# Two mixer layers: the gate projections in three float32r passes instead of plain float32

## The chip, the cores and the metric

One core of one Trainium2 chip. The time is the device time of one execution in microseconds (us), as a median over runs; lower is better. The engines are PE (TensorE, matrix products), DVE (VectorE), ACT (ScalarE), POOL (GpSimd) and SP (SyncE, which issues all transfers here).

## What is computed

A hybrid encoder trunk of two layers, 256 tokens of 1024 channels. Each layer is a SwiGLU FFN, then the mixers, then a second FFN. In the mixers one input projection feeds three branches (RWKV-7, Hyena long convolution, Mamba-2 SSD) and the gates:

```python
proj = h @ w_in
ya = rwkv7_mixer(proj[..., :o1], ...) @ pa_w
yb = hyena_mixer(proj[..., o1:o2], ...) @ pb_w
yc = ssd_mixer(proj[..., o2:o3], ...) @ pc_w
gates = jax.nn.sigmoid(proj[..., o3:]).reshape(bsz, L, N_BRANCH, D_MODEL)
merged = gates[:, :, 0] * ya + gates[:, :, 1] * yb + gates[:, :, 2] * yc
return merged @ w_out
```

## The kernel before

Activations lie with channels on the 128 partitions and tokens along the row, so 1024 channels are eight tiles of 128x256. A projection tile of 128 output channels is eight products, each with a 128x128 piece of a 512 KB weight tile. Per mixer layer there are 63 such tiles: 15 for RWKV, 12 for Hyena, 12 for SSD, 24 for the gates (eight per branch), and one narrow tile for SSD's dt.

There are two ways to multiply. `plain` loads a weight tile into the ring `raw` (four slots), and the product is float32; its two matmul records are named `psd<-hhi,raw`, since the input tiles carry the name `hhi`. `unit` loads into the same ring and then splits the weights into a high part `whi` (ACT, L279, two of 128x512) and a low part `wlo` (DVE, L309, two of 128x512, raw minus `whi`); `mm3` then makes three float32r passes: high by high, high by low, low by high. The FFN, the merges and the output projection use `unit`; all input projections of the mixers use `plain`. Not all of the tiles are made at the same place: the first few of a layer are made early, behind the preceding FFN.

The order on each engine comes from a scheduler that simulates the program and fills each in-order engine's queue; each engine then runs its own queue in that order, and waits on semaphores. `bank` and `dbank` give PSUM banks (`psd`, three of them, for projections; `psm` and `pss` for the rest).

`mixers` goes through RWKV first: `rw_proj` projects and shifts (the shifts on DVE read the bank twice, then it is free), `rw_keys` and `rw_scores` make scaled keys and masked score triangles for two pairs of heads (the masks are DVE multiplications with `cst`), which SP moves through DRAM (`zin`) into the layout in which `rw_invert` inverts them on POOL (some 60 operations, L919 and L921), and back (`zout`). `rw_chain` and `rw_out` then work with 32x32 and 64x64 matmuls that need the inverted triangles. Gate, dt and SSD tiles have no part in that chain, and the scheduler uses them to fill PE. A gate's result goes through ACT (`go`) to DRAM (`gate`) and comes back as `gi` at the merges. `merge` multiplies each branch by its weights and its gate, in the order 2 (SSD), 0 (RWKV), 1 (Hyena). A branch is split for `mm3` by `out_split` into `yx`. Buffers named `arena_0` and `arena_1` are one memory that `take` and `give` cut up; `arena_1` lies in the pool of the phase `q`, which ends with `rw_out(1)`, and the pools `wp` and `lp` open behind it.

## Time and profile before

| | before |
|---|---|
| median of 3 runs | 1668.75 us (1667.75 to 1669.92) |
| profiled execution | 1675.59 us, its span 1673.7 us |
| granted clock of PE, mean | 0.975 |
| busy PE / DVE / ACT / POOL | 94% / 69% / 48% / 16% |
| mixers' projections, layer 0 / layer 1 | about 258 to 565 us / 1073 to 1372 us |

Busy is the time in which an engine works on instructions, as a share of the span. An engine's idle time matters only where it lies in the chain that ends last.

### The profile page before, as it was taken

The page shows a single profiled execution, that of the slowest core. Times are in us where ns is not written, and L with a number is a line of the kernel's source. Part 1 is how long each engine was busy: PE and PEld are TensorE (multiplying, and loading weights), DVE is VectorE, ACT ScalarE, POOL GpSimd, SP SyncE. Part 2 cuts the span into 40 slices and gives each one's busy share as a digit, 9 for nine tenths or more (in the row PEclk, how much of TensorE's full clock was granted, in tenths as well). Part 3 has the DMA queues.
Part 4 walks back from the last instruction along what each step waited for, and adds up shares of the span by engine and source line. Part 5 has one row for each costly group of instructions (what it writes and reads, how often), then busy time and mean ns, then how long its engine had stood idle before and what let it go on. Part 6 is the DMA issues. An engine that isn't in the chain of part 4 may idle for free.

```text
span 1673.7 us, 31929 instructions
## 1 busy us (share of the span) xinstructions
PE 1569.5 (94%) x12118; PEld 1424.0 (85%) x12118; DVE 1150.0 (69%) x2326; ACT 801.3 (48%) x1566; POOL 267.4 (16%) x376
## 2 busy tenths in 40 slices
PE   5999999879998988899999999998999998989996
PEld 2999998768877878899999999877787787989996
DVE  6788856636446677888888887467454557876665
ACT  2655545423243535655575555452424342665554
POOL 0000013567001001100030000348620100030001
PEclk9999999989999999899999999998999999989998
DMA  9898834554548754788869986345555655666663
GB/s 376 305 324 280 282 123 155 129 127 144 169 150 288 242 170 151 282 304 295 266 220 366 315 307 199 120 106 138 156 151 158 223 188 194 189 198 221 222 177 93
DMA packets 157879, 355.74 MB, mean 213 GB/s; under 512 B 55900, under 2 KB 75805, under 8 KB 157470
## 3 DMA queue, kind: packets, MB, share of 16 engines
q1 hardware_dynamic: 157726, 353.71, 64.3%
q8 instruction: 95, 1.56, 0.4%
q14 instruction: 58, 0.48, 0.1%
HBM read 332.11 MB, written 18.91 MB: 210 GB/s over the span
## 4 chain that ended last, share of the span: by engine, by line
PE 66%; DVE 10%; POOL 9%; DMA 7%; ACT 4%; issue 3%; SPq 1%; DVEq 0%; ACTq 0%; POOLq 0%
PE psd L293 57%; PE psm L293 5%; PE pss L293 4%; POOL arena L921 3%; POOL arena L919 3%; DVE arena L282 3%; DVE arena L290 2%; DVE wlo L309 1%; SPq L296 1%; DMA arena<-in_ada 1%; ACT L279 1%; DMA gi<-gate 1%; DMA ada_raw<-in_ada 1%; ACT arena L279 1%; DMA raw<-in_pab 1%
## 5 line engine op out<-in xcount | busy, mean ns | idle before, releaser
L279 ACT ACTIVATE whi<-raw 128x512 fp32r<-128x512 f32 x608 | 370.6, 618 | 328.8 <-PE psd L293 268.2
L309 DVE TENSOR_TENSOR wlo<-raw,whi 128x512 fp32r<-128x512 f32 x608 | 405.1, 676 | 135.1 <-ACT whi L279 120.2
L293 PE MATMUL psd<-hhi,raw 128*128 128x256 f32 x1856 | 435.8, 389 | 0.7 <-DVE arena L290 0.7
L293 PEld LDWEIGHTS psd<-hhi,raw 128*128 128x128 f32 x1856 | 348.9, 192 | 63.3 <-issue 11.6
L293 PE MATMUL psd<-hhi,whi 128*128 128x256 f32 x1360 | 385.4, 285 | 9.9 <-DVE r L290 4.9
L293 PE MATMUL psd<-hhi,wlo 128*128 128x256 f32 x1360 | 384.6, 284 | 1.3 <-DVE wlo L309 1.3
L293 PE MATMUL psd<-hlo,whi 128*128 128x256 f32 x1360 | 385.5, 284 | 0.0
L293 PEld LDWEIGHTS psd<-hhi,whi 128*128 128x128 f32 x1360 | 262.0, 193 | 11.8 <-ACT sg L279 4.6
L293 PEld LDWEIGHTS psd<-hhi,wlo 128*128 128x128 f32 x1360 | 261.9, 193 | 1.6 <-DVE wlo L309 1.5
L293 PEld LDWEIGHTS psd<-hlo,whi 128*128 128x128 f32 x1360 | 262.5, 193 | 0.1
L293 PE MATMUL psd<-alo,whi 128*128 128x256 f32 x704 | 198.7, 282 | 0.0
L293 PE MATMUL psd<-ahi,wlo 128*128 128x256 f32 x704 | 197.8, 281 | 0.0
L293 PE MATMUL psd<-ahi,whi 128*128 128x256 f32 x704 | 197.4, 280 | 0.0
L581 POOL TENSOR_TENSOR r<-r,lmu 128x256 f32<-128x256 f32 x36 | 31.2, 899 | 1020.7 <-ACT lmu L279 841.3
L290 DVE SCALAR_TENSOR_TENSOR ada_raw<-ada_raw,cond 128x1024 f32<-128x1024 f32 x104 | 127.1, 1222 | 20.3 <-DMA ada_raw<-in_ada 20.1
L293 PEld LDWEIGHTS psd<-ahi,wlo 128*128 128x128 f32 x704 | 134.0, 190 | 0.3
L293 PEld LDWEIGHTS psd<-alo,whi 128*128 128x128 f32 x704 | 132.8, 189 | 0.2
L293 PEld LDWEIGHTS psd<-ahi,whi 128*128 128x128 f32 x704 | 132.2, 188 | 0.1
L293 PE MATMUL pss<-arena 128*64 128x128 f32 (+5 forms) x486 | 101.7, 385 | 26.9 <-ACT arena L279 8.6
L279 ACT ACTIVATE arena<-arena 128x512 f32<-128x512 f32 (+4 forms) x108 | 65.8, 619 | 102.5 <-DVE arena L290 35.6
L293 PEld LDWEIGHTS pss<-arena 128*64 128x64 f32 (+3 forms) x486 | 65.4, 195 | 52.1 <-issue 21.0
L293 PE MATMUL psm<-arena 32*32 32x32 f32 (+6 forms) x664 | 64.5, 263 | 28.1 <-DVE arena L290 12.6
(228 smaller groups left out, 2169.9 us busy)
## 6 DMA issues: line engine op xcount, KB each, us to landing
raw<-in_wi SPq DMA_DIRECT2D x176, 512.0 KB, 4.6
raw<-in_win SPq DMA_DIRECT2D x118, 512.0 KB, 3.8
ada_raw<-in_ada SPq DMA_DIRECT2D x104, 512.0 KB, 5.5
raw<-in_wo SPq DMA_DIRECT2D x64, 512.0 KB, 3.8
arena<-in_ada SPq DMA_DIRECT2D x32, 512.0 KB, 5.9
raw<-in_wo SPq DMA_DIRECT2D x32, 384.0 KB, 3.7
raw<-in_pab SPq DMA_DIRECT2D x24, 512.0 KB, 4.3
raw<-in_wout SPq DMA_DIRECT2D x16, 512.0 KB, 4.2
```

Of the source, the lines that this page charges most:

```text
L279: return self.nc.scalar.activation(out=out, in_=in_, func=func, **k)
L282: return self.nc.vector.tensor_tensor(out=out, in0=a, in1=b, op=op)
L290: return self.nc.vector.scalar_tensor_tensor(out=out, in0=a, scalar=s, in1=b, op0=op0, op1=op1, **k)
L293: return self.nc.tensor.matmul(out, lhsT, rhs, start=start, stop=stop, **k)
L296: self.nc.sync.dma_start(out, in_)
L309: return self.act(hi, src, AF.Copy), (eng or self.nc.vector).tensor_tensor(out=lo, in0=src, in1=hi.bitcast(F32), op=SUB)
L581: x = sub_(out=r[:, m, :], in0=r[:, m, :], in1=mu[:], op=SUB)
L919: g.tensor_tensor(out=tv, in0=zw[:, j + 1:32, j:j + 1].to_broadcast([64, n, j]), in1=zw[:, j:j + 1, 0:j].to_broadcast([64, n, j]), op=MUL)
L921: g.tensor_tensor(out=zw[:, j + 1:32, 0:j], in0=zw[:, j + 1:32, 0:j], in1=tv, op=ADD)
```

## The change

The 24 gate tiles of a layer go through `unit` and take three float32r passes over a split input. For that `h_part` splits the eight input tiles into `hlo` (the high part, on ACT) and `hl` (the low part, on DVE), in eight steps. It is written behind `rw_proj(l, 1)`. The SSD outputs stay whole (`sy0`, `sy1`) and are split when they are merged, as the other two branches were; `yx` moves from the pool `pp` to `lp`. All other tiles stay as they were.

```diff
@@ -685,17 +685,25 @@
         self.dense_pair(outs, ws, self.h)
         self.paired = dict(zip(ij, outs))
 
-    def proj(self, l, i):
+    def proj(self, l, i, parted=False):
         if i in self.ready:
             y, b = self.ready.pop(i)
             self.act(y, y, AF.Identity, bias=b)
             return y
         if i in self.paired:
             return self.paired.pop(i)
-        w = self.plain(self.ap["win"][l, i].rearrange("p k c -> p (k c)"))
+        w = (self.unit if parted else self.plain)(self.ap["win"][l, i].rearrange("p k c -> p (k c)"))
         p = self.dbank()
-        self.dense(p[:], w, self.h)
+        self.dense(p[:], w, self.hs if parted else self.h)
         return p
+
+    def h_part(self):
+
+        self.hs = []
+        for x in self.h:
+            hi, lo = self.t("hlo", 256, 8, F32R), self.pt("hl", 256, 8, F32R)
+            self.split(hi[:], lo[:], x)
+            self.hs.append((hi[:], lo[:]))
 
     def shift(self, l, dst, i, spread=False):
 
@@ -1082,7 +1090,7 @@
         self.ya.append(y)
 
     def out_split(self, y):
-        yx = self.pt("yx", [2, 2, 256], 2, F32R)
+        yx = self.lt("yx", [2, 2, 256], 2, F32R)
         self.split(yx[:, 0], yx[:, 1], y)
         return [(yx[:, 0, p, :], yx[:, 1, p, :]) for p in (0, 1)]
 
@@ -1194,7 +1202,7 @@
                             self.mm(py[64 * e:64 * e + 64, p, ts], xd[:, c, d, hs], ws[:, e, n, :], n == 0, n == 2)
                     F(f"sws{t}")
                 F("svb")
-            y = A("sy", 2, 256)
+            y = self.main.take(f"sy{g}", (2, 256))
             for p in (0, 1):
                 j = 2 * g + p
                 self.stt(y[:, p, :], self.sx[:, j, :], self.dh[:, j:j + 1], py[:, p, :], MUL, ADD)
@@ -1208,8 +1216,8 @@
             self.rsqrt(rs)
             for p in (0, 1):
                 self.stt(y[:, p, :], y[:, p, :], self.pc(l, "snw", 2 * g + p), rs, MUL, MUL)
-            self.yc += self.out_split(y)
-            F("scb", "sy", "ssq", "srs", "xd")
+            self.yc.append(y)
+            F("scb", "ssq", "srs", "xd")
 
 
     def hy_sin(self, x):
@@ -1342,7 +1350,7 @@
         for br in (2, 0, 1):
             self.gd[br] = self.dp.tile([128, 8, 256], F32, tag=f"gate{br}", bufs=2, name=f"gate{l}{br}")
             for m in range(8):
-                pg = self.proj(l, 39 + 8 * br + m)
+                pg = self.proj(l, 39 + 8 * br + m, True)
                 go = self.pt("go", 256, 2)
                 self.act(go[:], pg, AF.Tanh, scale=0.5)
                 self.dma(self.gd[br][:, m, :], go[:])
@@ -1372,7 +1380,7 @@
         A = self.A
         with self.phase("q") as pool:
             self.arena_open((self.pp, ARENA), (pool, AHEAD))
-            blk = self.arena.sub("blk", BLK)
+            self.main, blk = self.arena, self.arena.sub("blk", BLK)
             st = [None, None]
             self.gd, self.mh = [None] * 3, []
             self.relief = REL[0]
@@ -1383,6 +1391,7 @@
             self.rw_keys(st[0])
             self.rw_scores(st[0])
             st[1] = self.rw_proj(l, 1)
+            self.h_part()
             self.relief = REL[1]
             self.rw_invert(st[0])
             self.rw_keys(st[1])
@@ -1422,14 +1431,16 @@
                 self.ring = None
             self.mg = self.A("mg", 8, 256)
             self.relief = REL[4]
-            self.merge(l, 2, self.yc, True, False)
+            both = lambda ys: [x for y in ys for x in self.out_split(y)]
+            self.merge(l, 2, both(self.yc), True, False)
+            self.F("sy0", "sy1")
             with self.within(blk):
                 self.hyena(l)
             self.ln_begin(l, 1)
             wout = [self.ap["wout"][l, m].rearrange("p k c -> p (k c)") for m in range(8)]
             ws = [self.unit(u, ahead=NPRE) for u in wout[:NPRE]]
-            self.merge(l, 0, [x for y in self.ya for x in self.out_split(y)], False, False)
-            self.merge(l, 1, [x for y in self.yb for x in self.out_split(y)], False, True)
+            self.merge(l, 0, both(self.ya), False, False)
+            self.merge(l, 1, both(self.yb), False, True)
             self.F("y0", "y1")
             self.relief = REL[5]
             for m in range(8):
```

What moves on the engines, in layer 0. First DVE's start of the mixers: `psd_2963` to `psd_2966` are banks of the projections made early, and the `arena_0` rows are their shifts. Before:

```order
L286 TENSOR_SCALAR a0h_3129<-par_66 128x8
L290 SCALAR_TENSOR_TENSOR arena_0_3094<-psd_2963,par_66,arena_0_3094 128x255
L290 SCALAR_TENSOR_TENSOR arena_0_3094<-psd_2964,par_66,arena_0_3094 128x255
L290 SCALAR_TENSOR_TENSOR arena_0_3094<-psd_2963,par_66,arena_0_3094 128x255
L290 SCALAR_TENSOR_TENSOR arena_0_3094<-psd_2965,par_66,arena_0_3094 128x255
L290 SCALAR_TENSOR_TENSOR arena_0_3094<-psd_2964,par_66,arena_0_3094 128x255
L290 SCALAR_TENSOR_TENSOR arena_0_3094<-psd_2966,par_66,arena_0_3094 128x255
```

and in the changed kernel:

```order
L286 TENSOR_SCALAR a0h_3129<-par_66 128x8
L309 TENSOR_TENSOR hl_3491<-hhi_3029,hlo_3490 128x256
L309 TENSOR_TENSOR hl_3495<-hhi_3032,hlo_3494 128x256
...
L309 TENSOR_TENSOR hl_3519<-hhi_3050,hlo_3518 128x256
L290 SCALAR_TENSOR_TENSOR arena_0_3094<-psd_2963,par_66,arena_0_3094 128x255
L290 SCALAR_TENSOR_TENSOR arena_0_3094<-psd_2964,par_66,arena_0_3094 128x255
L290 SCALAR_TENSOR_TENSOR arena_0_3094<-psd_2965,par_66,arena_0_3094 128x255
L290 SCALAR_TENSOR_TENSOR arena_0_3094<-psd_2966,par_66,arena_0_3094 128x255
L290 SCALAR_TENSOR_TENSOR arena_0_3094<-psd_2963,par_66,arena_0_3094 128x255
L290 SCALAR_TENSOR_TENSOR arena_0_3094<-psd_2964,par_66,arena_0_3094 128x255
```

The eight `hl` rows now stand ahead of the first shift, and the second shift of `psd_2963` is the fifth instead of the third. On ACT the eight `hlo` stand between and behind the rows that make the input tiles, ahead of the first row of the work that follows (`wab`):

```order
L279 ACTIVATE hhi_3044<-r_2099,mod_938 128x256
L279 ACTIVATE hlo_3502<-hhi_3038 128x256
L279 ACTIVATE hlo_3506<-hhi_3041 128x256
L279 ACTIVATE hhi_3047<-r_2099,mod_938 128x256
L279 ACTIVATE hhi_3050<-r_2099,mod_938 128x256
L279 ACTIVATE hlo_3510<-hhi_3044 128x256
L279 ACTIVATE hlo_3514<-hhi_3047 128x256
L279 ACTIVATE hlo_3518<-hhi_3050 128x256
L279 ACTIVATE wab_3052<-psd_2963 128x2
L279 ACTIVATE wab_3056<-psd_2964 128x2
```

before, three rows of `hhi` stood there, and then `wab`. Second, DVE at the score masks of the first pair of heads (`psm_3269` and `pss_3270`, then `psm_3281` and `pss_3282`). Before:

```order
L282 TENSOR_TENSOR arena_1_3095<-arena_0_3094,arena_1_3095 128x512
L290 SCALAR_TENSOR_TENSOR arena_1_3095<-arena_0_3094,arena_1_3095 64x8x64 x4
L282 TENSOR_TENSOR arena_1_3095<-psm_3269,cst 128x512
L282 TENSOR_TENSOR arena_1_3095<-pss_3270,cst 128x512
L282 TENSOR_TENSOR arena_1_3095<-psm_3281,cst 128x512
L282 TENSOR_TENSOR arena_1_3095<-pss_3282,cst 128x512
L282 TENSOR_TENSOR arena_1_3095<-psm_3330,cst 128x512
```

and in the changed kernel:

```order
L282 TENSOR_TENSOR arena_1_3095<-arena_0_3094,arena_1_3095 128x512
L290 SCALAR_TENSOR_TENSOR arena_1_3095<-arena_0_3094,arena_1_3095 64x8x64 x4
L309 TENSOR_TENSOR wlo_4510<-raw_4507,whi_4509 128x512
L309 TENSOR_TENSOR wlo_4514<-raw_4507,whi_4513 128x512
L309 TENSOR_TENSOR wlo_4548<-raw_4545,whi_4547 128x512
L309 TENSOR_TENSOR wlo_4552<-raw_4545,whi_4551 128x512
L282 TENSOR_TENSOR arena_1_3095<-psm_3269,cst 128x512
L282 TENSOR_TENSOR arena_1_3095<-pss_3270,cst 128x512
L309 TENSOR_TENSOR wlo_4586<-raw_4583,whi_4585 128x512
L282 TENSOR_TENSOR arena_1_3095<-psm_3281,cst 128x512
L282 TENSOR_TENSOR arena_1_3095<-pss_3282,cst 128x512
L282 TENSOR_TENSOR arena_1_3095<-psm_3330,cst 128x512
```

Five `wlo` of the gates' weights (tiles `raw_4507`, `raw_4545`, `raw_4583`) have come in ahead of the second pair of masks. Fifteen more stand between the masks and the end of the second pair's scores. Third, PE at the first matmuls that need the first inversion (32x32, `psm_3846` before, `psm_3878` in the changed kernel). `psd_4618` and `psd_4890` are the dt tile, `psd_4654` and `psd_4926` the first SSD tile. Before:

```order
L293 MATMUL psd_4618<-hhi_3050,raw_4616 64x256
L293 MATMUL psd_4654<-hhi_3029,raw_4652 128x256
...
L293 MATMUL psd_4654<-hhi_3038,raw_4652 128x256
L293 MATMUL psm_3846<-arena_1_3095 32x32 x2
L293 MATMUL psd_4654<-hhi_3041,raw_4652 128x256
L293 MATMUL psd_4654<-hhi_3044,raw_4652 128x256
L293 MATMUL psm_3846<-arena_1_3095 32x32 x30
```

and in the changed kernel:

```order
L293 MATMUL psd_4860<-hl_3519,whi_4856 128x256
L293 MATMUL psm_3839<-cst,arena_0_3094 64x64 x16
L293 MATMUL psd_4860<-hlo_3518,wlo_4857 128x256
L293 MATMUL psd_4890<-hhi_3029,raw_4888 64x256
...
L293 MATMUL psd_4926<-hhi_3029,raw_4924 128x256
...
L293 MATMUL psd_4944<-hhi_3029,raw_4942 128x256
...
L293 MATMUL psd_4962<-hhi_3029,raw_4960 128x256
...
L293 MATMUL psd_4962<-hhi_3035,raw_4960 128x256
L293 MATMUL psm_3878<-arena_1_3095 32x32
...
L293 MATMUL psd_4962<-hhi_3038,raw_4960 128x256
L293 MATMUL psm_3878<-arena_1_3095 32x32 x31
```

Ten gates and the dt tile stand ahead of them in both; of the SSD tiles half of the first before, two and three eighths of the third now. Last, ACT where the SSD outputs are split. Before, among the operations of `rw_chain`:

```order
L279 ACTIVATE arena_0_3094<-arena_0_3094 128x256
L279 ACTIVATE yx_4939<-arena_0_3094 128x512
L279 ACTIVATE go_5159<-psd_5150 128x256
...
L279 ACTIVATE arena_0_3094<-psd_5260,par_66 128x256
L279 ACTIVATE yx_5033<-arena_0_3094 128x512
L279 ACTIVATE arena_0_3094,mod_5065<-arena_0_3094 128x1024
```

and in the changed kernel, behind `rw_out(1)`'s last `arena_1` rows and among the first transforms of Hyena (L1309):

```order
L1309 COPY arena_0_3094<-pss_6225 128x512
L279 ACT_TABLE_LOAD
L279 ACTIVATE arena_1_3095<-arena_1_3095 128x512
L1309 COPY arena_0_3094<-pss_6231 128x512
L279 ACT_TABLE_LOAD
L279 ACTIVATE arena_1_3095<-arena_1_3095 128x512
L279 ACTIVATE arena_0_3094<-arena_0_3094,par_66 128x256 x2
L279 ACTIVATE yx_6051<-arena_0_3094 128x512
L279 ACTIVATE yx_6054<-arena_0_3094 128x512
L279 ACTIVATE wqh_6302<-raw_6300 128x512
```

Both splits have moved behind the end of `rw_out(1)`, and PE's products of merge 2 with them.

## Rows read from the trace of the kernel before

**Rows 1.** The page: busy time, and the chain by engine and line.

```profile
PE 1569.5 (94%) x12118; PEld 1424.0 (85%) x12118; DVE 1150.0 (69%) x2326; ACT 801.3 (48%) x1566; POOL 267.4 (16%) x376
...
PE 66%; DVE 10%; POOL 9%; DMA 7%; ACT 4%; issue 3%; SPq 1%; DVEq 0%; ACTq 0%; POOLq 0%
PE psd L293 57%; PE psm L293 5%; PE pss L293 4%; POOL arena L921 3%; POOL arena L919 3%; DVE arena L282 3%; DVE arena L290 2%; DVE wlo L309 1%; SPq L296 1%; DMA arena<-in_ada 1%; ACT L279 1%; DMA gi<-gate 1%; DMA ada_raw<-in_ada 1%; ACT arena L279 1%; DMA raw<-in_pab 1%
```

**Rows 2.** Busy time of engines in the two stretches of projections.

```profile
258.00:565.00 307.00, 282.50 (x2193) 230.64 (x2192) 172.46 (x353) 119.56 (x239) 102.42 (x148) 0.97 0.56 172
1073.00:1372.00 299.00, 283.83 (x2189) 231.49 (x2189) 161.21 (x337) 116.84 (x232) 96.91 (x146) 0.97 0.54 161
```

**Rows 3.** PE's waits from 243 to 420 us: total, times, longest.

```profile
PE psm L293 <- DVE arena L290: 8.2, 2, 5.1
PE psm L293 <- DMA arena<-zin: 5.8, 1, 5.8
```

**Rows 4.** Busy time of engines from 400 to 540 us.

```profile
400.00:540.00 140.00, 134.51 (x1174) 109.11 (x1172) 75.74 (x192) 48.04 (x95) 16.28 (x27) 1.00 0.59 189
```

**Rows 5.** Timeline of ACT: start, duration, instruction; banks of two plain tiles.

```profile
266.80 0.47 ACT L279 ACTIVATE arena<-psd,c 128x256 f32<-128x256 f32 x1 [2.98 <-PE psd L293]
...
270.25 0.47 ACT L279 ACTIVATE arena<-psd,c 128x256 f32<-128x256 f32 x1 [2.25 <-PE psd L293]
```

**Rows 6.** Timeline of PE in the second FFN: float32r passes, five steps apart.

```profile
687.73 0.28 PE L293 MATMUL psd<-hhi,wlo 128*128 128x256 f32 x1
...
688.33 0.28 PE L293 MATMUL psd<-hlo,whi 128*128 128x256 f32 x1
```

**Rows 7.** Costliest groups of the page: the weight splits of today.

```profile
L279 ACT ACTIVATE whi<-raw 128x512 fp32r<-128x512 f32 x608 | 370.6, 618 | 328.8 <-PE psd L293 268.2
L309 DVE TENSOR_TENSOR wlo<-raw,whi 128x512 fp32r<-128x512 f32 x608 | 405.1, 676 | 135.1 <-ACT whi L279 120.2
```

**Rows 8.** Timeline of ACT and DVE at the mixers' start.

```profile
250.62 1.09 ACT L279 ACTIVATE hhi<-r,mod 128x256 f32<-128x256 f32 x2 [0.26 <-DVE r L282]
251.62 0.27 ACT L279 ACTIVATE wab<-psd 128x2 f32<-128x2 f32 x3
257.08 0.18 DVE L290 SCALAR_TENSOR_TENSOR c<-par 128x15 f32<-128x15 f32 x1 [0.81 <-DMA xd<-r]
...
258.10 3.22 DVE L290 SCALAR_TENSOR_TENSOR arena<-psd,par,arena 128x255 f32<-128x255 f32 x8 [0.39 <-ACT arena L279]
```

**Rows 9.** Timeline of DVE: masks of the first pair of heads.

```profile
298.53 0.69 DVE L282 TENSOR_TENSOR arena<-psm,cst 128x512 f32<-128x512 f32 x1
...
299.73 0.69 DVE L282 TENSOR_TENSOR arena<-psm,cst 128x512 f32<-128x512 f32 x1
```

**Rows 10.** DMA issues of the page: KB each, median us to landing.

```profile
raw<-in_win SPq DMA_DIRECT2D x118, 512.0 KB, 3.8
```

**Rows 11.** Timeline of POOL: one shape of the inversion at two places.

```profile
326.69 1.34 POOL L919 TENSOR_TENSOR arena<-arena 64x150 f32<-64x150 f32 x1
...
381.64 0.48 POOL L919 TENSOR_TENSOR arena<-arena 64x150 f32<-64x150 f32 x1
```

**Rows 12.** Timeline of PE and DVE around merge 2.

```profile
565.38 0.59 PE L293 MATMUL psd<-yx,whi 128*128 128x256 f32 x2
...
579.22 1.04 PE L1300 MATMUL pss<-cst,arena 128*128 128x128 f32 x8
...
585.83 2.74 PE L293 MATMUL pss<-arena 128*128 128x512 f32 x6
...
604.30 8.28 PE L293 MATMUL pss<-arena 128*128 128x256 f32 x24 [3.92 <-DVE gi L290]
576.05 0.68 DVE L282 TENSOR_TENSOR arena<-arena,psm 128x512 f32<-128x512 f32 x1
```

**Rows 13.** Timeline of SP: copies of `zin` of pair 1, and `zout`.

```profile
355.29 3.71 SPq L296 DMA_DIRECT2D arena<-arena  x5
...
366.08 0.79 SPq L296 DMA_DIRECT2D zout<-arena  x2
```

## The prediction

> **What bounds the kernel now.** I read first the page's busy times and its chain of work [rows 1]: PE is busy for 94% of the span and carries 66% of the chain, `psd L293` (the projection products) alone 57%, while the chain also has 9% on POOL and 10% on DVE. So the kernel is PE's, but with pieces in which something else ends last. Next the two stretches in which the 48 changed tiles lie [rows 2]: PE works 282.5 of 307 us in layer 0 and 283.8 of 299 us in layer 1, DVE 172 and 161, ACT 120 and 117. PE therefore idles 24.5 and 15.2 us inside them, and the next question is where. The table of waits of PE between 243 and 420 us [rows 3] answers: 8.2 us for DVE's `arena` and 5.8 us, in one piece, for `arena<-zin`, the return of the inverted triangles that POOL makes in `rw_invert`. From 400 to 540 us PE is busy 134.5 of 140 us [rows 4]. The reader should see two parts in each layer: one up to about 378 us in which DVE, SP and POOL pass work along a chain and PE fills the holes with gates, and one behind it in which PE alone counts.
>
> **What a gate tile gives.** Plain products: ACT takes one tile's bank at 266.80 and the next one's at 270.25 us [rows 5], 3.45 us a tile of eight products. Three float32r passes: two starts that are five passes apart, 687.73 and 688.33 us, give 0.12 us a pass [rows 6], so 24 of them are 2.88 us. The gain is 0.57 us a tile, 13.7 us a layer, 27.4 us in all.
> The Trainium skill (FP8 and Floating Point Precision, TensorE Precision Notes) counts a true FP32 product as four passes through the array. By that rule three passes would save a quarter of 3.45 us, 0.86 us a tile, 41 us in all. The rows measure a ratio of 2.88 to 3.45, not 3 to 4, and I go by them.
>
> **What a gate tile costs elsewhere.** Two `whi` activations of 618 ns and two `wlo` subtractions of 676 ns [rows 7]: 24 tiles add 29.7 us to ACT and 32.4 us to DVE per layer. DVE would stand at about 204 of 307 us and ACT at 149 [rows 2], so neither becomes the bound of the stretch as a whole. From 400 us on their work lies beside PE's and costs nothing, as the order puts the splits of the later gates at least a tile or two ahead of their products; if that cover were gone, each late `wlo` would cost PE up to its 0.68 us. The harm is where DVE is in the chain.
>
> **(a) Start of the mixers, +4.4 us a layer.** In the new order eight `hlo` activations stand among and behind the `hhi` ones, and eight `hl` subtractions ahead of the first shifts. ACT: the nearest row is two `hhi` in 1.09 us [rows 8], about 0.4 us for an unscaled copy; five of the eight fit into the idle time that ACT has between its `hhi`, three stand behind the last one, ahead of `wab` at 251.62: +1.1 us. DVE: eight tensor-tensor of 128x256, priced by the eight shifts of nearly that size in 3.22 us [rows 8], so about 3.0 us; its wait of 0.39 us ahead of them goes. Then the second shift of the tile `psd_2963`, which gives PE its next bank, is fifth instead of third: 0.8 us. Sum 4.5, less a little slack: 4.4 us (bounds: 3 us if the 0.81 us wait [rows 8] hides ACT's share, 7 us if nothing hides).
>
> **(b) The score masks of head pair 0, +5.9 us.** Their DVE rows start at 298.53 and 299.73 us [rows 9] with no idle time, at the end of a stretch in which DVE is full. Now four `wlo` stand ahead of the first mask pair and a fifth ahead of the second. Four are 2.4 us at the 0.6 us spacing of these rows. The fifth is of tile G2, whose `raw` slot is one of four and comes free only behind a `wlo` of the same queue: load 3.8 us [rows 10], `whi` 0.62, `wlo` 0.68, counted from the second `wlo`, end about 5.9 us behind the old mask. The masks feed `zin` and so the inversion. Bounds: 3.4 us if the load is early, 7 if SP is late with it.
>
> **(c) POOL's inversion, +1.5 us.** POOL takes 1.34 us for a 64x150 operation at 326.69, while DVE works on two SBUF inputs, and 0.48 us for the same shape at 381.64 [rows 11]. Some 15 more `wlo` lie in `rw_keys(1)` and `rw_scores(1)`, about 9 us. If all of them fell into the inversion and POOL ran at half speed under them it would lose 4.5 us; part of them stand where DVE waited and the inversion may be over before: between 0 and 4.5, I take 1.5, as DVE was already full in much of that stretch.
> The Trainium skill (SBUF — State Buffer, Who interferes with whom) says that a DVE instruction with two SBUF inputs blocks a GpSimd instruction that reads SBUF until it is done. The trace agrees in sign, 1.34 against 0.48 us. By the rule at its hardest every one of the 15 blocks POOL for its whole length, 9 us; the sum here goes without it.
>
> So the event for which PE waited 5.8 us comes D = 4.4 + 5.9 + 1.5 = 11.8 us later.
>
> **(d) What PE has left behind that event.** Before, ten gates, the dt tile and half of the first SSD tile (`psd_4654`) stood ahead of the first 32x32 matmuls; now the ten gates are cheaper by 5.7 us, and two SSD tiles and three eighths of the third are ahead, 1.875 more: 1.875 x 3.45 = 6.5 us. PE's work ahead of the event is thus the same as before, and it waits longer. Behind it there are 6.5 us less of SSD tiles and 14 gates, 14 x 0.57 = 8.0 us: 14.5 us less. Net per layer 11.8 - 14.5 = -2.7 us.
>
> **(e) The merges, +1 us.** `yx` now sits in the pool of phase l, in memory that `rw_out(1)` still uses, so both SSD splits stand behind the last `arena_1` operation. Before, merge 2 started at 565.38 us and the last addition of `rw_out(1)` ended at 576.7 [rows 12]. Now merge 2 waits for it, and PE has ahead of it, as before, two groups of `rw_out(1)`'s own matmuls, and newly the hyena transposes (1.04 us) and the first forward transforms (2.74 us and a few more) [rows 12], which I estimate at some 7 us together. Of the 11 us about 4 are left bare, and the transposes and transforms done early are not work added. Against them stands the wait of 3.92 us at 604.30 for `gi` [rows 12], part of which the later start may absorb, and DVE's lighter load while `rw_out(1)` ends. Bounds -2 to +6, I take +1.
>
> **Sum.** Two layers of -2.7 + 1 = -1.7: -3.4 us. The profiled execution took 1675.6 us (span 1673.7) and the runs' median is 1668.75, so the trace is 0.4% long; a difference of a few us carries over unscaled. 1668.75 - 3.4 = 1665 us. 0.2%, 3.3 us, is about what a measurement here can tell from no change.
>
> **Rivals.**
> - *The chain has slack (A).* If the masks' wait is hidden, because the loads arrive early and PE fills the time with gates, only (a) is lost: -27.4 + 2 x 4.4 = -18.6, 1650 us. For it: PE is the bound of [rows 1], 57% by this kind of line. Against it: 5.8 us of idle time at the event [rows 3], which any delay adds to.
> - *Merge 2 waits bare (B), slower.* Place: between the last projection and hyena. Price +6 us a layer, when `rw_out(1)` is late by its own DVE work and the transforms don't fill: 2 x (-2.7 + 6) = +6.6, 1675 us. It decides from 2.7 us of bare wait on. For it: `rw_out(1)` and merge 2 overlap now by 11 us. Against it: the forward transforms were moved up.
> - *Inversion 1 and `zout` share SP's queue (C), slower.* The copies of `zin` of pair 1 now stand ahead of `zout(0)`; in layer 0 the last group of them was issued from 355.29 and `zout(0)` at 366.08 [rows 13]. Later by 15 `wlo`, 9.8 us, they use up nearly all of the 7 us that were between (355.29 + 3.71 to 366.08): 2 to 5 us a layer more, and with c at 4.5 D is 17 to 20: 2 x (-14.5 + 18.5 + 1) = +10, 1679 us. It decides at D above 13.5.
> - *No change at all (N).* The gains and the delays cancel to under 3 us by other sizes of b and c: 1668.
>
> **How the numbers follow.** Forecast 0.40 (own range 1656 to 1675, from b and c at their ends: half of it faster, 0.20, a quarter the same), A 0.24, B 0.17, C 0.12, N 0.07. Faster by over 0.2%: 0.20 + 0.24, and 0.01 of N: 0.45. Same: 0.10 + 0.07 + 0.03 of the rivals: 0.20. Slower 0.35. The range leaves about one in ten on each side: 1648, a little below A, to 1681, above C.
>
> **What would show it.** Gates in the after trace with 0.12 us between passes and 2.9 us a tile (else the gain is wrong); the first tile behind the paired ones 4 us later in each layer; the masks behind a `wlo` that waits for ACT and DMA; PE's wait at the event near 13 us instead of 5.8 (PE's own stream starts 4.4 us later too); POOL's inversion within 2 us of its old length; and PE's start of merge 2 behind the last addition of `rw_out(1)`. I would be wrong above all if PE's wait at the event did not grow (then A), or if merge 2 left PE idle by more than 3 us (then B).

## The result

The changed kernel takes 1678.73 us (median of 5 runs, 1675.48 to 1684.72), the kernel before 1667.93 us beside it (1667.71 to 1669.92): a ratio of 1.0064, interval 1.0049 to 1.0078. It is 0.6% slower, where 0.2% faster was forecast. Its profiled execution is run 1 of the five, 1680.49 us, span 1678.7.

Busy time in the page of the changed kernel:

```profile
PE 1559.5 (93%) x12502; PEld 1434.8 (85%) x12502; DVE 1224.9 (73%) x2438; ACT 859.2 (51%) x1678; POOL 277.2 (17%) x376
```

PE is busy 10 us less than before [rows 1], and yet the time is longer. To see where it went, both traces are cut at three places in each layer: the start of the paired tiles (`psm<-hhi,raw`), the first 32x32 matmul behind the first inversion, and the end of the last plain tile. The kernel before, PE's timeline (start, duration, instruction, idle time before it and what ended it):

```profile
251.86 6.42 PE L293 MATMUL psm<-hhi,raw 128*128 128x256 f32 x29
...
373.85 0.64 PE L293 MATMUL psm<-arena 32*32 32x32 f32 x4 [5.79 <-DMA arena<-zin]
...
563.41 2.32 PE L293 MATMUL psd<-hhi,raw 128*128 128x256 f32 x10
...
1066.01 4.26 PE L293 MATMUL psm<-hhi,raw 128*128 128x256 f32 x19
...
1185.67 0.21 PE L293 MATMUL psm<-arena 32*32 32x32 f32 x2 [1.02 <-issue]
...
1366.93 5.78 PE L293 MATMUL psd<-hhi,raw 128*128 128x256 f32 x26
```

The changed kernel, the same places, with the first tile behind the paired ones and the start of merge 2 besides:

```profile
251.16 7.07 PE L293 MATMUL psm<-hhi,raw 128*128 128x256 f32 x32
...
261.91 3.33 PE L293 MATMUL psd<-hhi,raw 128*128 128x256 f32 x7 [3.67 <-DVE arena L290]
...
394.24 0.21 PE L293 MATMUL psm<-arena 32*32 32x32 f32 x2 [1.15 <-DMA arena<-zout]
...
562.62 5.34 PE L293 MATMUL psd<-hhi,raw 128*128 128x256 f32 x24
...
580.15 0.72 PE L293 MATMUL psd<-yx,whi 128*128 128x256 f32 x4 [2.33 <-ACT yx L279]
...
1067.30 7.07 PE L293 MATMUL psm<-hhi,raw 128*128 128x256 f32 x32
...
1077.88 2.40 PE L293 MATMUL psd<-hhi,raw 128*128 128x256 f32 x10 [3.51 <-DVE arena L290]
...
1207.29 0.24 PE L293 MATMUL psm<-arena 32*32 32x32 f32 x2
...
1373.35 5.34 PE L293 MATMUL psd<-hhi,raw 128*128 128x256 f32 x24
```

From the paired tiles to the 32x32 matmuls: 121.99 us before and 143.08 after in layer 0, 119.66 and 139.99 in layer 1, so 21.1 and 20.3 us more, where the prediction had D = 11.8. From there to the end of the last plain tile (start plus duration of its row): 18.2 and 15.6 us less, where it had 14.5. The rest of the merges is 1.5 and 2.1 us longer (last `yx` product at 623.48 and 1429.87 before, 627.22 and 1437.94 after). Together +4.4 and +6.8, 11.2 us, about what the runs show (10.8). Between the two traces as a whole there are only 5 us, because the trace of before spent some 6 us more outside these stretches than the trace of the changed kernel; the cuts inside the mixers are not touched by that.

The chain of layer 0 ahead of the 32x32 matmuls, changed kernel, DVE at the first masks (the `psm,cst` row is a mask):

```profile
303.54 3.79 DVE L309 TENSOR_TENSOR wlo<-raw,whi 128x512 fp32r<-128x512 f32 x4
307.25 0.68 DVE L282 TENSOR_TENSOR arena<-psm,cst 128x512 f32<-128x512 f32 x1
...
309.59 0.69 DVE L309 TENSOR_TENSOR wlo<-raw,whi 128x512 fp32r<-128x512 f32 x1 [1.07 <-ACT whi L279]
```

SP, the first `zin`, the last copies of pair 1's triangles and `zout`:

```profile
310.91 0.71 SPq L296 DMA_DIRECT2D zin<-arena  x1
...
379.99 5.83 SPq L296 DMA_DIRECT2D arena<-arena  x5
385.87 1.06 SPq L296 DMA_DIRECT2D zout<-arena  x2
```

POOL, first and last operation of the first inversion:

```profile
330.79 0.25 POOL L927 TENSOR_TENSOR arena<-arena 64x30 f32<-64x30 f32 x1 [13.03 <-DMA arena<-zin]
...
381.57 0.24 POOL L929 TENSOR_TENSOR arena<-arena 64x30 f32<-64x30 f32 x1
```

The four `wlo` ahead of the masks take 3.7 us, and the fifth waits 1.07 us for its `whi`; the mask that began at 298.53 [rows 9] begins at 307.25. The inversion lasts 51.0 us; before it was 46.3 us, from 319.72 to 366.06. It ends at 381.81, and `zout` leaves only at 385.87: SP's queue stands until 385.82 at pair 1's copies (for some 2 us of that it waits for the landing of earlier ones). Before, `zout` left 0.02 us behind the end [rows 13].

PE had troubles of its own in this stretch. Its waits from 243 to 420 us in the changed kernel (in total, times, longest) now have two rows for splits of the gates:

```profile
PE psd L293 <- DVE wlo L309: 5.4, 5, 2.3
...
PE psd L293 <- ACT whi L279: 2.4, 1, 2.4
```

and the granted clock is lower. Busy time from the start of the paired tiles to the 32x32 matmuls (us, then PE, PEld, DVE, ACT, POOL busy, then the granted clock, of which 1.00 is 2.4 GHz and a value below it a part at 1.2), kernel before and changed kernel:

```profile
251.86:373.85 121.99, 106.40 (x621) 87.41 (x620) 69.93 (x111) 52.67 (x110) 64.50 (x87) 0.95 0.50 138
251.16:394.24 143.08, 121.83 (x732) 103.32 (x731) 95.84 (x150) 68.39 (x143) 68.64 (x87) 0.87 0.45 124
```

By the prediction's reckoning PE has as much to do ahead of the matmuls as before, more SSD tiles against cheaper gates. But it is busy for 15.4 us more and idle for 5.7 us more (8.3 and 12.0 in layer 1). The ten gates, counted from the start of one pass to the next with the waits taken out, take 39.0 us, 0.16 us a pass and not 0.12, as many of them run at 1.2 GHz and then start 0.21 us apart; 8.1 us of waits come on top. So ahead of the inversion a three-pass gate is no cheaper than a plain tile.

The first 10 us behind the first wait show one such fall of the clock: window of layer 0 before, of layer 0 in the changed kernel, of layer 1 in the changed kernel.

```profile
260.00:270.00 10.00, 10.00 (x48) 8.81 (x47) 4.14 (x11) 3.59 (x9) 1.36 (x2) 1.00 0.69 238
260.00:270.00 10.00, 8.09 (x25) 6.74 (x26) 5.55 (x15) 2.22 (x5) 0.00 (x0) 0.66 0.37 125
1076.00:1086.00 10.00, 8.12 (x38) 7.20 (x39) 5.52 (x15) 3.16 (x8) 0.00 (x0) 1.00 0.47 169
```

PE had waited 0.69, 3.67 and 3.51 us ahead of them. The clock fell in the second and not in the third, so such a wait is not always followed by a fall.

### The profile page after: what moved, and what is told of

Read it like the earlier page. It is cut to its first block, busy times and chain, and to the rows that moved or that the text cites. A ratio compares the mean times of both kernels' runs of the same rounds, so it can differ in the third digit from the quotient of the medians.

```text
span 1678.7 us, 33023 instructions
## 1 busy us (share of the span) xinstructions
PE 1559.5 (93%) x12502; PEld 1434.8 (85%) x12502; DVE 1224.9 (73%) x2438; ACT 859.2 (51%) x1678; POOL 277.2 (17%) x376
## 5 line engine op out<-in xcount | busy, mean ns | idle before, releaser
L279 ACT ACTIVATE whi<-raw 128x512 fp32r<-128x512 f32 x704 | 430.4, 620 | 392.5 <-PE psd L293 323.1
L309 DVE TENSOR_TENSOR wlo<-raw,whi 128x512 fp32r<-128x512 f32 x704 | 482.0, 695 | 178.6 <-ACT whi L279 162.2
L293 PE MATMUL psd<-hlo,whi 128*128 128x256 f32 x1744 | 504.0, 290 | 4.9 <-ACT whi L279 4.9
L293 PEld LDWEIGHTS psd<-hlo,whi 128*128 128x128 f32 x1744 | 341.4, 196 | 9.8 <-ACT whi L279 5.6
L293 PE MATMUL psd<-hhi,raw 128*128 128x256 f32 (+1 forms) x1088 | 254.2, 391 | 7.4 <-DVE arena L290 7.2
L293 PEld LDWEIGHTS psd<-hhi,raw 128*128 128x128 f32 (+1 forms) x1088 | 206.0, 193 | 43.6 <-issue 12.0
L290 DVE SCALAR_TENSOR_TENSOR ada_raw<-ada_raw,cond 128x1024 f32<-128x1024 f32 x104 | 127.3, 1224 | 15.3 <-DMA ada_raw<-in_ada 15.1
L293 PE MATMUL psd<-hlo,wlo 128*128 128x256 f32 x384 | 118.5, 310 | 11.8 <-DVE wlo L309 11.8
L293 PE MATMUL psd<-hl,whi 128*128 128x256 f32 x384 | 115.7, 302 | 0.0
```

Source lines behind the costliest of these rows:

```text
L279: return self.nc.scalar.activation(out=out, in_=in_, func=func, **k)
L290: return self.nc.vector.scalar_tensor_tensor(out=out, in0=a, scalar=s, in1=b, op0=op0, op1=op1, **k)
L293: return self.nc.tensor.matmul(out, lhsT, rhs, start=start, stop=stop, **k)
L309: return self.act(hi, src, AF.Copy), (eng or self.nc.vector).tensor_tensor(out=lo, in0=src, in1=hi.bitcast(F32), op=SUB)
```

## The experiments

Theory 1 is that the chain alone costs: the splits on DVE and SP's queue bring the first inversion late, and what PE saves behind it does not pay for that. Theory 2 is that PE itself comes late to the inversion, through waits for splits and the lower clock. Theory 3 is that the merge part costs. Times are given with the ratio to the kernel before that was run beside them and its 95% interval.

**The first ten gates plain.** `h_part` is moved behind `rw_scores(st[1])`, and its instructions are held there.

```diff
+            self.rw_scores(st[1])
+            self.h_part()
...
-                pg = self.proj(l, 39 + 8 * br + m, True)
+                pg = self.proj(l, 39 + 8 * br + m, n >= 10)
+                n += 1
```

> The first ten gate tiles of each layer stay plain float32, only the last 14 take three passes, and the input is split behind the second pair's score masks; the merge part stays as in the change. Theory 1 (the chain: the splits on DVE and SP's queue bring the first inversion 20 us later, and that is given back only in part): the first 32x32 matmuls of layer 0 come back to about 374 us (changed kernel 394, before 374), 14 x 0.57 = 8 us a layer stay, less 1 us for the merge, about 1654 us. Theory 2 (PE itself: gate products ahead of the inversion wait for their own splits and PE runs more of that stretch at the lower clock): the same here, about 1654 us, since both causes go; what tells them apart are the other runs. Theory 3 (the merge part costs): 1664 us or more. If three passes gave nothing on PE: about 1669 us.

Measured: 1643.67 us, 0.985 (0.983 to 0.987), 25 us below the kernel before and the fastest kernel of this study. That is 10 us below what both theories expected; 5 us of them is the merge part, which the run with the merge part alone shows to be a gain. PE at the first 32x32 matmul of layer 0:

```profile
374.47 0.70 PE L293 MATMUL psm<-arena 32*32 32x32 f32 x4 [5.66 <-DMA arena<-zin]
```

That is 121.2 us behind the paired tiles, as before. It shows that the loss lies in the first ten gates and the place of the input's split, and that the change without them pays; theories 1 and 2 remain.

**The input's split behind the shifts.** Order only:

```diff
-            self.split(hi[:], lo[:], x)
+            i, j = self.split(hi[:], lo[:], x)
+            self.after(i, self.sha)
+            self.after(j, self.shs)
```

> The change with only the split of the input held behind the shifts of the first projections (its 8 ACT and 8 DVE instructions stand later, nothing else is told to move). Theory 1: the chain starts some 5 us earlier in each layer (zin of layer 0 at 306 instead of 310.9 us, first 32x32 matmuls at 389 instead of 394.2), time 2 x 4 to 5 us below the changed kernel, about 1670 us. Theory 2: PE is late by its own work as well, and the first 32x32 matmuls move by the 2.3 us of the first tile and what the clock gives back, 1673 to 1676 us. Theory 3: no change, 1678 us.

Measured: 1674.27 us, 1.0033 (1.0019 to 1.0047), about 5 us below the changed kernel (the ratios differ by 0.0031). The way from the paired tiles to the 32x32 matmuls is 138.8 and 136.9 us, 4.3 and 3.1 shorter. The way lies between the two theories, nearer to theory 1's 5 us than to theory 2's 2.3; the time is within theory 2's 1673 to 1676 us.

**The merge part alone**, on the kernel before (the lines of the diff that concern `sy` and `yx`).

> The kernel before with the merge part alone: SSD outputs kept whole and split when they are merged, yx in the pool of phase l; gates plain, no split of the input. Theories 1 and 2: within 3 us of the kernel before, 1668 to 1671 us, with merge 2 starting some 10 us later and the end of the merges at most 2 us later. Theory 3: most of the loss is here, 1675 us or more.

Measured: 1664.3 us, 0.997 (0.995 to 0.999): 5 us faster than the kernel before. Theory 3 falls. The time is won, for the most part, between the 32x32 matmuls and the last plain tile, 186.4 and 185.5 us instead of 191.9 and 187.0; from there to the end of the merges it is 59.1 and 57.9 us, 1 us longer. The SSD splits no longer stand among the operations of `rw_chain`; that this is the reason is likely and not shown.

**The first masks ahead of the gates' low parts.** Order only, for the first eight gates; `hold` is the last mask of `rw_scores(st[0])`:

```diff
+            i, j = self.split(hi[:, 0:n], lo[:, 0:n], raw[:, o:o + n], self.nc.gpsimd if pool else self.nc.vector)
+            if self.hold:
+                self.after(j, self.hold)
```

> The change with the weights' low parts of the first gate tiles held behind the last score mask of the first pair of heads on DVE (order only). Theory 1: zin of layer 0 goes out some 5 to 6 us earlier than in the changed kernel (305 instead of 310.9 us), so does the inversion, and the time falls by 2 x 5 us to about 1668 us. Theory 2: the inversion is earlier but PE comes to it late by its own waits for splits and by the lower clock, the first 32x32 matmuls move by 0 to 2 us, and the time stays at 1674 to 1679 us.

Measured: 1670.02 us, 1.0001 (0.998 to 1.002), 10.5 us below the changed kernel. SP's first `zin`:

```profile
301.81 0.70 SPq L297 DMA_DIRECT2D zin<-arena  x1
```

and PE's first 32x32 matmul:

```profile
382.22 0.22 PE L294 MATMUL psm<-arena 32*32 32x32 f32 x2 [0.66 <-DMA arena<-zout]
```

`zin` is 40.9 us behind the first tile (260.93), as in the kernel before, and the 32x32 matmuls come 11.0 us sooner behind the paired tiles (6.1 us in layer 1) than in the changed kernel. This is as theory 1 had it: behind the paired tiles `zin` is 8.1 and 5.7 us earlier than in the changed kernel, and SP's queue holds `zout` for 1.4 and 0.9 us only. Moving these low parts gives back as much as the changed kernel lost to the kernel before. They are not the whole loss: the 32x32 matmuls are still 10.1 and 14.2 us later than before, and what PE saves behind them now pays for that. In layer 1 they begin without a wait, so PE is the later one there.

**Pair 1's copies from ACT's queue.**

```diff
+            q = nc.scalar if w and d else nc.sync
```

> The change with the transfers of the second half of pair 1's score triangles issued from ACT's queue instead of SP's, so that zout of the first inversion no longer queues behind them. Theory 1 (the chain alone sets the loss): zout goes out 4 us earlier (382 instead of 385.9 us in layer 0), the first 32x32 matmuls at 390 instead of 394.2, 1670 us. Theory 2 (PE comes to the inversion late by its own waits and the lower clock; it arrived at 393.1 in the changed kernel): the first 32x32 matmuls move by about 1 us, 1675 to 1678 us.

Measured: 1684.77 us, 1.0091 (1.006 to 1.012), by the ratios 4.5 us above the changed kernel, with intervals that overlap. ACT's queue in layer 0, pair 1's copies and ACT's own copy behind them:

```profile
383.07 2.93 ACTq L296 DMA_DIRECT2D arena<-arena  x4
386.04 1.96 ACT L932 COPY arena<-arena 64x1024 f32<-64x1024 f32 x1 [3.91 <-DMA arena<-arena]
```

The first half of `zout` goes 0.9 us behind POOL's end (382.87 behind 381.94). The second half needs ACT's copy (L932), and that stood behind ACT's own DMA issues until 386.04; it leaves at 388.02. The wait has changed its queue; the run tells nothing between the theories, and why layer 0 is longer behind that (177.6 us to the last plain tile instead of 173.7) is open.

**Pair 1's copies from POOL's queue**, behind the last operation of the inversion (`q = nc.gpsimd`, held by `after`).

> The change with the transfers of the second half of pair 1's score triangles issued from POOL's queue, behind the last operation of the first inversion, so that neither SP nor ACT holds zout back. Theory 1 (the chain): zout follows POOL's end at once (382 instead of 385.9 us in layer 0), the first 32x32 matmuls at 390, and the time falls by 2 x 3.5 us to 1671 us; the second inversion starts some 5 us later, which nothing waits for. Theory 2 (PE comes late by itself, it arrived at 393.1): the first 32x32 matmuls stay at 393, time 1676 us or more.

Measured: 1675.9 us, 1.0037 (1.002 to 1.005), some 4 us below the changed kernel by the ratios. SP in layer 0, the two halves of `zout`, and ACT's copy that the second half needs:

```profile
382.55 0.80 SPq L296 DMA_DIRECT2D zout<-arena  x2
...
387.25 0.77 SPq L296 DMA_DIRECT2D zout<-arena  x2
...
385.28 1.94 ACT L935 COPY arena<-arena 64x1024 f32<-64x1024 f32 x1
```

PE, the first 32x32 matmul:

```profile
393.52 0.25 PE L293 MATMUL psm<-arena 32*32 32x32 f32 x4
```

The first half of `zout` follows POOL at once, 0.03 us behind 382.52. The second is hardly earlier than in the changed kernel (387.25 to 387.44), as ACT's copy stood behind four copies of `rw_chain` and a `go`. So in layer 0 the run takes only half of SP's wait away. Still the 32x32 matmuls begin at 393.52 with no wait in their row: PE had just finished the SSD products ahead of them, as it had at 393.09 in the changed kernel. So theory 2 holds there: with PE's work in this order, the chain alone can win at most a little over 1 us at this place. In layer 1, where both halves of `zout` go in time, 2 us were won (137.96 us instead of 139.99), again with no wait.

**All three held** (input's split, masks, pair 1's copies on ACT's queue).

> The change with all three held: the input's split behind the first shifts, the first gates' low parts behind the first pair's masks, and the second half of pair 1's triangles on ACT's queue. What is left of the delay is POOL's longer inversion, about 5 us. Theory 1: the first 32x32 matmuls of layer 0 at about 379 us, and 4.8 us (input's split alone) + 10.7 us (masks alone) + some 3 us below the changed kernel: about 1660 us. Theory 2: PE, which waits for the splits of the gates in that stretch, sets the rest: 1665 to 1670 us, no better than the masks alone.

Measured: 1662.94 us, 0.9962 (0.995 to 0.998). That is 17 us below the changed kernel, the sum of the first two alone is 15.7; theory 1 (1660 us) came nearer. But

```profile
382.16 0.24 PE L294 MATMUL psm<-arena 32*32 32x32 f32 x2
```

shows no wait either, here nor in layer 1: PE finished the work ahead at that moment. From the paired tiles it is still 131.0 us, 9 more than before. Along the chain POOL's inversion (51.6 us) is 5.3 of them and a wait of `zout` 1.0; the last 2.8, between `zout` and the matmuls, are PE's.

**The first ten gates without their low weight parts.** These gates' values lack the low term; all 24 keep their three passes.

```diff
+            if self.short:
+                self.act(hi[:, 0:n], raw[:, o:o + n], AF.Copy)
+                parts.append((hi, hi))
+                continue
```

> The change, all 24 gates in three passes, with the low weight parts of the first ten gate tiles of each layer left out (their high part stands in for it, so these gates' values lose that term): 20 DVE subtractions a layer fewer, everything else issued as in the change. If these subtractions on DVE are the loss (masks, POOL, waits of PE): the inversion is back at 46 us, the first 32x32 matmuls near 378, and the time at or below the version with ten plain gates, 1638 to 1645 us. If the three passes ahead of the inversion are worth nothing anyway, since PE waits for the inversion there: 1645 to 1650 us, the late version plus the 4.8 us of the input's split. If something else is the loss: above 1655 us.

Measured: 1661.3 us, 0.9936 (0.991 to 0.996). First and last operation of POOL's inversion:

```profile
323.52 0.24 POOL L932 TENSOR_TENSOR arena<-arena 64x30 f32<-64x30 f32 x1 [11.27 <-DMA arena<-zin]
...
369.57 0.24 POOL L934 TENSOR_TENSOR arena<-arena 64x30 f32<-64x30 f32 x1
```

It is back at 46.3 us in layer 0, so the low parts were its extra 4.7 us there; in layer 1 it is 47.2, 3.9 of the 5.9. The time is that of the third case, in which something else is part of the loss. The 32x32 matmuls are 129.8 and 132.0 us behind the paired tiles. The input's split still delays the start, and `zout` leaves at 373.33, 3.5 us behind POOL's end. SP:

```profile
363.16 4.52 SPq L297 DMA_DIRECT2D arena<-arena  x5
...
368.37 4.86 SPq L297 DMA_DIRECT2D gate<-go  x3
```

It isn't pair 1's copies that hold it here: without the low parts they are through at 367.68, 2.1 us ahead of POOL's end. The third of three transfers of gate results stands in the queue ahead of `zout` and waits 3.6 us for its `go` on ACT. So the low parts on DVE are most of what made pair 1's copies late, and a gate's transfer can hold `zout` as well.

**DVE work of the same length without gates.** On the merge part alone, 15 instructions per layer between those of `rw_keys(1)` and `rw_scores(1)`; their results are not used. First subtractions with two SBUF inputs:

```diff
+            self.prev = self.nc.vector.tensor_tensor(out=o[:], in0=self.fa, in1=self.fb, op=SUB)
```

> The merge part alone (gates plain) plus 15 DVE subtractions of 128x512 of two constant SBUF tiles per layer, put between the DVE instructions of the second pair's keys and scores; their results are not used. It stands for the gates' low parts there, without their weights, waits or passes. If DVE instructions with two SBUF inputs slow POOL's inversion: 51 us instead of 46.4, the first 32x32 matmuls 5 us later than in the merge part alone (377.5 instead of 372.6), time 1664 + 2 x 4 = 1672 us. If the longer inversion in the changed kernel had another cause: 46 us and 1664 to 1667 us.

Measured: 1683.33 us, 1.0074 (1.006 to 1.009), 19 us above the merge part alone (17 by the ratios) and 11 above what was expected. POOL:

```profile
318.64 0.24 POOL L931 TENSOR_TENSOR arena<-arena 64x30 f32<-64x30 f32 x1 [12.94 <-DMA arena<-zin]
...
368.92 0.24 POOL L933 TENSOR_TENSOR arena<-arena 64x30 f32<-64x30 f32 x1
```

The inversion lasts 50.5 us (50.4 in layer 1). Then reductions, which read one SBUF tile:

```diff
+            self.prev = self.nc.vector.tensor_reduce(out=o[:, 0:1], in_=self.fa, axis=mybir.AxisListType.X, op=ADD)
```

> As the run with 15 subtractions, but with 15 reductions of 128x512 to 128x1, which read one SBUF tile, in their place: the same DVE time at the same places. If it is the second SBUF input that slows POOL: the inversion stays at 46 us and the time at 1664 to 1667 us. If any DVE work there delays the chain (by the second pair's scores): as slow as with the subtractions, 1672 us.

Measured: 1678.06 us, 1.0046 (1.003 to 1.006), 14 us above the merge part alone (13 by the ratios), and above both values that were expected. POOL, first and last operation of the inversion:

```profile
319.57 0.24 POOL L931 TENSOR_TENSOR arena<-arena 64x30 f32<-64x30 f32 x1 [10.76 <-ACT arena L280]
...
366.24 0.24 POOL L933 TENSOR_TENSOR arena<-arena 64x30 f32<-64x30 f32 x1
```

SP behind it:

```profile
366.51 0.80 SPq L307 DMA_DIRECT2D zout<-arena  x2
367.41 0.60 SPq L307 DMA_DIRECT2D zin<-arena  x1
...
376.44 3.95 SPq L307 DMA_DIRECT2D arena<-zout  x8
```

The inversion is 46.9 us (46.5). A reduction also writes one column only, where a subtraction writes 512. That the second SBUF input slows POOL, and not the writing, can be read in the changed kernel, where a mask writes 512 columns from one SBUF tile and one PSUM bank. DVE and POOL, beside two `wlo` and beside a mask:

```profile
357.60 2.17 DVE L309 TENSOR_TENSOR wlo<-raw,whi 128x512 fp32r<-128x512 f32 x2
358.26 0.95 POOL L927 TENSOR_TENSOR arena<-arena 64x238 f32<-64x238 f32 x1
...
368.70 0.67 DVE L282 TENSOR_TENSOR arena<-pss,cst 128x512 f32<-128x512 f32 x1
368.77 0.59 POOL L927 TENSOR_TENSOR arena<-arena 64x228 f32<-64x228 f32 x1
```

In the second inversion, with little beside it, these two shapes take 0.60 and 0.58 us. The `wlo` are slowed as well: two in 2.17 us, where one alone takes 0.68.

The time is still far up. SP shows why: the second half of pair 1's copies, made late by DVE, now stands from 367.41 between `zout` and its way back, `arena<-zout`, which begins 123.5 us behind the paired tiles instead of 117.7 in the merge part alone. The 32x32 matmuls come 13.0 us behind `zout`, there 7.7. At these matmuls the two harms are about equal: the reductions, which hardly slow POOL, bring them 5.1 and 7.1 us later than the merge part alone, and the subtractions another 5.2 and 4.9.

**Only the last seven gates in three passes** (`n >= 17` in the first experiment).

> The late version with only the last seven gate tiles in three passes instead of the last 14. If each tile behind the first inversion gives the same on PE: half way between the merge part alone (1664.3) and the late version (1643.7), 1654 us. By 0.57 us a tile alone: 1644 + 2 x 7 x 0.57 = 1652 us. If the late version's gain is mostly of another kind (order of the work): 1645 us or less, or 1664.

Measured: 1659.73 us, 0.9937 (0.992 to 0.996), between the values that were expected. Against the merge part alone seven tiles a layer bring 4.6 us, and the next seven 16 (5.5 and 14.5 by the ratios, each good to some 5 us). By the passes alone each seven should bring 8 us. The sum for 14, 20.6 us against 16, is of the right size; by these figures the last seven bring less than the seven ahead of them, and as each version has another order, the passes need not be the reason.

**Hyena's 12 tiles in three passes too**, on the first experiment.

```diff
-        p = self.proj(l, i)
+        p = self.proj(l, i, wn == "hcw")
```

> The late version (first ten gates plain, last 14 in three passes, input's split behind the second masks) with Hyena's 12 input tiles in three passes too. If behind the first inversion PE alone counts, 2 x 12 x 0.57 = 13.7 us less than the late version: 1630 us. If DVE and ACT, which get 16 us and 15 us more a layer, delay the second pair's chain or the side work there: 1640 to 1648 us.

Measured: 1665.54 us, 0.9969 (0.995 to 0.999), 22 us above the late version (20 by the ratios) and worse than all that was expected. PE's waits from 500 to 570 us, in total, times, longest:

```profile
PE psd L293 <- DVE arena L290: 5.2, 3, 2.9
PE psm L293 <- ACT arena L1017: 3.5, 1, 3.5
```

PE waits 5.2 us for banks that DVE's L290 operations free late, and 3.5 us for a copy of `rw_chain` on ACT, which stood behind a table load and an activation that waited for DVE. The late version has neither of the two waits in this stretch. They are part of the loss; the rest of it, and layer 1, I did not follow.

## Why the prediction was wrong

The step that failed is D, the delay of the first inversion, in the part on POOL and SP: (c) had POOL lose 1.5 us where it lost 4.7 and 5.9, and `zout`'s wait in SP's queue, 4.0 and 3.5 us, was priced as a rival and left out of the sum. The sum had 11.8 us, the trace 21.1 and 20.3. A second step failed beside it: that PE would come early to the event and wait 13 us there.

| step, us a layer | forecast | measured, layer 0 / 1 |
|---|---|---|
| (a) start, to the first tile | 4.4 | 3.0 / 3.6 |
| (b) first tile to `zin` | 5.9 | 8.2 / 5.7 |
| (c) POOL's inversion | 1.5 | 4.7 / 5.9 |
| `zout` behind pair 1's copies on SP | 0 | 4.0 / 3.5 |
| small rest (`zin` to POOL, `zout` to PE) | 0 | 1.2 / 1.6 |
| (d) behind the event, to the last plain tile | -14.5 | -18.2 / -15.6 |
| (e) merges | +1 | +1.5 / +2.1 |
| net | -1.7 | +4.4 / +6.8 |

- (a) and (b) were right in mechanism and about right in size. Taken away alone they brought 5 and 10.5 us over both layers (expected from my terms: 8.8 and 11.8). Inside (b) two errors cancelled, which is luck: the four `wlo` took 3.7 us and not 2.4, and the fifth added 1.7 and 2.0 and not 3.5. The 5.9 us isn't exact by its own figures either, which give 5.1 to 6.3. In layer 0 (b) was 2.5 us longer than in layer 1, and the clock is the likely reason: with `wlo` ahead of the masks, first tile to `zin` takes 49.0 to 49.2 us in the four mixer layers whose clock fell to 1.2 GHz for 6.8 us at the first wait (layer 0 of the changed kernel and of the run from ACT's queue, both layers of the run from POOL's), 47.7 in the one with 3.4 us of it, and 46.3 to 46.6 in the three with none.
- (c) was mis-sized, and the bound of 4.5 us was too low. I took half speed under 9 us of low parts for the bound; the runs give 4.7 to 5.9 us with 15 of them, 4.2 us and 5.2 us with 15 subtractions and nothing else, and 0.6 to 1.2 us with 15 one-input instructions. Thirteen of the 15 fell into the inversion, and they took 13.9 us there and not 9, since POOL slows DVE too (0.69 us each behind the inversion). The rule of the Trainium skill (SBUF — State Buffer, Who interferes with whom), that a DVE instruction contends with a GpSimd one that reads SBUF if it has two SBUF inputs and not if it has one, agrees with these two runs in kind. The hardest reading that I gave it, 9 us, was too much.
- SP's queue was in the text as rival C, with its place and the price (D of 17 to 20, 1679 us), and was given 0.12. The case came out: D of 20 to 21 and 1678.7 us. That the time fits to 1 us is partly luck, as D was larger than the rival had it and (d) gave back more. What I got wrong is the weight. I had the slack of 7 us in [rows 13] and the 9.8 us by which the low parts move pair 1's copies in the same paragraph, so that the collision was to be expected, not a mishap. Pair 1's copies end 27.5 us later behind the paired tiles than before (359.0 to 385.82, less the two starts) and POOL 16.4 us (366.06 to 381.81), so that 11.1 us met a slack of 7.1. Without gates and with little of POOL's loss, 15 reductions cost 13 to 14 us, mostly by SP's order, though at another place of it, between `zout` and its way back.
- (d) held behind the event: less what the merge part alone wins there (5.4 and 1.5 us), the trace has 12.7 and 14.1 us where the sum had 14.5. Two passes of the changed kernel that lie 24 passes, a whole tile, apart start 2.83 us apart, 0.12 us a pass:

```profile
469.83 0.28 PE L293 MATMUL psd<-hl,whi 128*128 128x256 f32 x1
...
472.66 0.28 PE L293 MATMUL psd<-hl,whi 128*128 128x256 f32 x1
```

  For 14 tiles a layer the forecast gave 16 us, and 20.6 were measured over the merge part alone. By the four-pass rule of the Trainium skill (FP8 and Floating Point Precision, TensorE Precision Notes) an estimate is 24 us. The run with seven tiles shows that a tile's share varies too much to tell the two apart by time; the 0.12 us of these rows beside the 3.45 us of a plain tile [rows 5] speak for the smaller gain. Ahead of the event the 5.7 us that ten gates were to save did not come: they took 3.9 us a tile without their waits.
- (e) came out near its value (merge 2 began at 580.15 with a wait of 2.33 us for `yx`), but the merge part as a whole is a gain of 5 us, which I had not seen. It is part of the larger (d).
- PE's own lateness was not in the sum at all. I let PE wait 13 us at the event; it waited 1.15 in layer 0 and not at all in layer 1. My sign for rival A, a wait that doesn't grow, came out without rival A: the wait shrank because PE was late too, and not because the chain had slack. PE's work ahead of the event was stretched by waits for splits (7.8 us in the two rows) and by the lower clock (0.87 instead of 0.95), so that PE and the chain arrive together, which the run from POOL's queue shows. In layer 0 of the changed kernel PE's work was done at 393.09 us and the transfers at 394.24, so how D divides between the two is open. The event's row in [rows 3] I also misread: `arena<-zin` carries pair 1's triangles to POOL, and the return is `arena<-zout`, which the changed kernel's row names.

## What to carry to other kernels

A cheaper operation that needs preparation on another engine is only cheap where that engine is off the path: the same change, applied to the 14 tiles behind the long serial stage and not to the ten ahead of it, and with the input's split moved behind that stage too, turned 0.6% slower into 1.5% faster. Before adding work to an engine that feeds a chain, follow each of its later outputs into every in-order queue and compare the slack there with the added time; here 7 us of slack on SP met 11 us. Look also at the engine that seems to wait: here PE's idle time at the event was gone once its own work waited for splits. The order came from a scheduler's estimates, and three changes of order and queue brought back 17 us.

## What the hardware showed

DVE work slows a POOL operation by what it reads: 15 subtractions of two SBUF tiles took the inversion from 46.4 to 50.5 us, 15 reductions of one SBUF tile left it at 46.9, and masks that read one SBUF tile and one PSUM bank left single operations as long as in the second inversion (0.59 us beside a mask, 0.58 there). The slowing goes both ways: `wlo` took 0.68 us alone and mostly 1.0 to 1.2 us beside POOL. PE's granted clock fell at some waits of 2 to 4 us and not at others: 0.66 in the window that follows 3.67 us of waiting, 1.00 behind 3.51 us in layer 1 and behind 0.69 us before.
